# Where the split weight tiles stand, and when the adaLN transfers are issued: one edit to a macaron transformer block

## The chip, the core and the metric

One NeuronCore of a Trainium2 chip runs the whole kernel. The metric is the device time of one execution in microseconds (us); the time before is the median of three runs, 1954.19 us (1942.38, 1954.19 and 1956.5). In the profile PE is TensorE, PEld its weight loads, DVE VectorE, ACT ScalarE, SP the engine whose queue issues the transfers.

## What is computed

One layer for 256 tokens of width 2048, in float32:

```python
mod = silu(c) @ w_ada + b_ada
sh1, sc1, gt1, sh2, sc2, gt2, sh3, sc3, gt3 = split(mod, 9)
h = x + 0.5 * gt1 * swiglu(modulate(rms_norm(x, g_ffn1), sh1, sc1), w1_gate, w1_up, w1_down)
nrm = modulate(rms_norm(h, g_mix), sh2, sc2)
q, k, v = split(nrm @ w_qkv, 3)          # 16 heads of 128: 8 neighbourhood, 8 dilated
...                                      # rms_norm of q and k, attention, rms_norm of the outputs
h = h + gt2 * (concat(o_na, o_dil) @ w_o)
h = h + 0.5 * gt3 * swiglu(modulate(rms_norm(h, g_ffn2), sh3, sc3), w2_gate, w2_up, w2_down)
```

The inner width of both feed-forward parts is 5632 (44 blocks of 128). `w_ada` has 9 x 2048 columns; the kernel calls a block of 128 of them one adaLN item, so there are 144 items of 1 MB.

## The kernel before

**The weight stream.** All large weights come in one fixed order as chunks of 128 x 1024 float32 (512 KB): 12 chunks w1_s, then w1_a (36), w1_b (80), w1_d (64), w1_c (48), w1_e (24), w_qkv (96), w_o (32), w2_a (64), w2_b (64), w2_d (64), w2_c (48), w2_e (24). Letters a, b and c are pieces of the gate and up projections, d and e of the down projection. `wraw` (L138) issues the transfer of a chunk into one of 5 buffers `rw`. For all but the 12 chunks w1_s, `wsplit` (L145) then makes two tiles of it: `hi`, a rounded copy made by ACT (L150), and `lo`, the rest, made by DVE (L151: raw minus hi). Each has 4 buffers (`LOB`), taken in turn. The four `hi` buffers stand one behind another in SBUF, then a spare tile `far` of 192 bytes, then the four `lo` buffers. A buffer has 4096 bytes a partition, so the `lo` of a chunk always stands 4 x 4096 + 192 = 16576 bytes behind its `hi`.

**The matmuls.** In the feed-forward parts and in w_o a chunk holds 8 blocks of 128 x 128. For each, `mm2` (L154) issues a pair of matmuls: `hi` as the stationary operand against 512 columns (an activation's own hi and lo side by side, L156), and `lo` against 256 columns (L157). A chunk is thus 8 pairs. In w_qkv the activations are stationary and the weights move: 12 matmuls of 512 columns a chunk (L162). The order of the instructions on PE is the program's.

**The adaLN items.** `ada_issue` (L119) issues the 1 MB transfer of an item into one of 3 buffers (two `ra`, one `rx`; two in the attention part), `ada_use` (L128) is one DVE instruction over 128 x 2048 (L131) that makes one column of `mods`. Items wait in the list `bg`. `W.chunk` (L296), which fetches three chunks ahead (`AHEAD`), adds `ws.rate` to a credit at each chunk and issues an item for each full credit: `RA` = 0.475 in w1_a, the four numbers of `RB` in w1_b, w1_d, w1_c and w1_e, `RQ` in w_qkv and w_o, `RE` in w2_a, `RF` in the pieces of the second feed-forward part. `bg_until(0)` (L405) stands ahead of w1_e and w2_e: all items have to be issued and used before it in the program. The framework schedules all engines but PE's hand-ordered part: within what data and buffers allow, it may move an instruction forwards or back in its engine's queue, the transfers on SP too.

**Waits.** DVE, ACT and SP each take their queue in order. An `ada_use` whose transfer hasn't landed holds up all that stands behind it on DVE, the `lo` of the next chunk among it.

Of the kernel before, what the change touches and what calls it, by code (L numbers as in the profile page):

```python
# [22 lines left out]
HD = 128  # L23
EPS = 1e-6
NEG = -1e30
CW = 1024
# [10 lines left out]
QS = 1  # L37
PACT = 0
RA = 0.475
RB = (0.1, 0.5, 0.4, 0.15)  # L40
RQ = 0.33
RE = 0.25
RF = (0.1, 0.2, 0.1, 0.1)
AHEAD = 3
# [3 lines left out]
LOB = 4  # L48
URGENT = 400
LINE = 16  # L50
MANUAL = {mybir.EngineType.PE}


# [10 lines left out]
def build(tc, a):  # L64
    nc = tc.nc
    with ExitStack() as ctx:
# [37 lines left out]
        cb = cp.tile([P, D], F32, name="cb")  # L104
        mods = [cp.tile([P, KT], F32, tag=f"m{j}", name=f"m{j}") for j in range(9)]
        nx = [cp.tile([P, 2, S], F32R, tag=f"nx{k}", name=f"nx{k}") for k in range(KT)]

        wide = {}
        turn = [0]
        hold = []  # L110

        def held(ins):
            if hold:
                tc.add_manual_dep(
                    ins.ins, hold[-1].ins.name,
                    mybir.DependencyInfo(mybir.DependencyClass.NoSync, mybir.DependencyReason.DATA),
                    reason="hold")

        def ada_issue(i):  # L119
            turn[0] += 1  # L120
            if wide and turn[0] % (ARA + ARX) >= ARA:
                raw = wide["p"].tile([P, D], F32, tag="arx", bufs=ARX, name=f"rx{i}")
            else:
                raw = wp.tile([P, D], F32, tag="ara", bufs=ARA, name=f"ra{i}")
            nc.sync.dma_start(raw, a["w_ada"][i])
            return raw

        def ada_use(raw, i):  # L128
# [8 lines left out]

        def wraw(src):  # L138
            raw = wp.tile([P, CW], F32, tag="raw", bufs=RAWB, name="rw")
            nc.sync.dma_start(raw, src)  # L140
            return raw

        far = []

        def wsplit(raw):  # L145
            hi = wp.tile([P, CW], F32R, tag="whi", bufs=LOB, name="hiw")
            if not far:
                far.append(wp.tile([P, 3 * LINE], F32, tag="far", bufs=1, name="far"))
            lo = wp.tile([P, CW], F32R, tag="wlo", bufs=LOB, name="low")
            nc.scalar.copy(hi, raw)  # L150
            nc.vector.tensor_tensor(lo, raw, hi.bitcast(F32), ALU.subtract)  # L151
            return hi, lo
# [120 lines left out]
        for nm in ("w1_s", "w1_a", "w1_b", "w1_d", "w1_c", "w1_e", "w_qkv", "w_o",  # L273
                   "w2_a", "w2_b", "w2_d", "w2_c", "w2_e"):
            first[nm] = len(srcs)
            srcs += [a[nm][c] for c in range(a[nm].shape[0])]

        class W:
            def __init__(self):
# [6 lines left out]

            def fetch(self, n):
                while self.head < n:
                    self.ready[self.head] = wraw(srcs[self.head])
                    self.head += 1  # L290

            def whole(self):
# [2 lines left out]

            def chunk(self, ahead=AHEAD):  # L296
                while self.head <= min(self.tail + ahead, len(srcs) - 1):
                    self.ready[self.head] = wsplit(wraw(srcs[self.head]))
# [77 lines left out]
        def ffn(kx, part, ready_k, gate, rates, stat=None, out=None):  # L376
# [120 lines left out]
        hps.close()  # L497

        with tc.tile_pool(name="att", bufs=2) as ap_, tc.tile_pool(name="atc", bufs=1) as ac:
            gq = ac.tile([P, 4, HD], F32, name="gq")  # L500
            nc.sync.dma_start(gq, a["qkg"].partition_broadcast(P))
            rope = ac.tile([P, 2, 2, 32], F32, name="rope")
            nc.sync.dma_start(rope, a["rope"])
            lnc = ac.tile([P, 2, S], F32, name="lnc")
# [18 lines left out]
            def at(u, fn):  # L523
                slots.setdefault(u, []).append(fn)
# [12 lines left out]
                s_["rr"] = rstd_from(s_["ss"], HD, 8, "rq")  # L537

            def qk_norm(g, j, nm, ps, t, s_):
                gi = j + (0 if g < 2 else 2)  # L540
                xn = ap_.tile([P, 4, HD], F32, tag=f"{nm}n{t}", bufs=1, name=f"{nm}n{t}")
                for i in range(4):
                    nc.vector.scalar_tensor_tensor(
                        xn[:, i, :], ps[t][:, i * P : (i + 1) * P],
                        s_["rr"][:, t * 4 + i : t * 4 + i + 1], gq[:, gi, :], ALU.mult, ALU.mult)
# [308 lines left out]
```

## Time and profile before

| what | value |
|---|---|
| median of three runs | 1954.19 us |
| profiled execution, its own time | 1967.14 us |
| its span, first to last instruction | 1965.4 us |
| mean granted TensorE clock | 0.992 |
| PE / DVE / ACT busy | 98% / 80% / 46% of the span |
| bytes moved, mean rate | 503.98 MB, 256 GB/s |

The four runs shown, the profiled one included, lie 25 us apart. Stages in the profile, by the first matmul of each: w1_a from 68 us, w1_b from 181, w1_d from 408, w1_c from 586, w1_e from 727, w_qkv from 802, w_o with the last heads from 1103, w2_a from 1221, w2_b from 1401, w2_d from 1581, w2_c from 1760, w2_e from 1894. A wait is shown as the engine and line that waited, what released it, the sum in us, how often, and the longest. A table by stretches of time counts the instructions that lie in each stretch, those cut by its ends included.

### The profile page before, as it was taken

How to read it: one execution, taken by the hardware profiler on the slowest of the kernel's cores; microseconds unless marked ns; L12 is line 12 of the kernel's file. 1: busy time of each engine (PE TensorE's matmuls, PEld its weight loads, DVE VectorE, ACT ScalarE, POOL GpSimd, SP SyncE). 2: the span in 40 equal slices, each digit the busy share in tenths (PEclk: the TensorE clock that was granted, in tenths of full speed). 3: DMA queues.
4: the chain of work that ended last, by engine and by line, in shares of the span. 5: the costliest groups of instructions: out<-in, count | busy, mean ns of one | idle time of the engine just before them, and what ended most of it. 6: DMA issues, size and time to landing. Idle time of an engine off the chain costs nothing.

```text
span 1965.4 us, 27570 instructions
## 1 busy us (share of the span) xinstructions
PE 1923.0 (98%) x10564; PEld 1659.7 (84%) x10564; DVE 1570.2 (80%) x2122; ACT 906.5 (46%) x1333; POOL 0.7 (0%) x6
## 2 busy tenths in 40 slices
PE   7999999999999999999999999999999999999999
PEld 5878888888887888887888788888888888888888
DVE  7799999998888867989766799988899865555565
ACT  2444544443333454545554555544455443334442
POOL 0000000000000000000000000000000000000000
PEclk8999999999999999999999999999999999999999
DMA  9988888899998976698655445899976666666664
GB/s 383 360 323 296 310 304 306 301 314 337 350 336 322 330 238 202 206 336 306 219 163 165 152 134 170 317 317 334 324 263 191 192 186 189 187 188 188 188 199 133
DMA packets 120083, 503.98 MB, mean 256 GB/s; under 512 B 13328, under 2 KB 15632, under 8 KB 101520
## 3 DMA queue, kind: packets, MB, share of 16 engines
q1 hardware_dynamic: 119952, 502.24, 75.2%
q8 instruction: 82, 1.34, 0.3%
q14 instruction: 49, 0.40, 0.1%
HBM read 500.09 MB, written 2.10 MB: 256 GB/s over the span
## 4 chain that ended last, share of the span: by engine, by line
PE 86%; DVE 7%; DMA 3%; issue 2%; ACT 2%; SPq 0%; DVEq 0%; ACTq 0%
PE pb L156 22%; PE pd L156 15%; PE pb L157 11%; PE pa L156 9%; PE pd L157 7%; PE pqv L162 5%; PE pa L157 5%; PE pqk L162 4%; DVE low L151 3%; PE pa L455 2%; PE pqq L162 2%; DMA ra<-in_w_ada_dram 2%; PE pso L156 2%; DVE ra L131 1%; DMA rx<-in_w_ada_dram 1%
## 5 line engine op out<-in xcount | busy, mean ns | idle before, releaser
L150 ACT CAST hiw<-rw 128x1024 fp32r<-128x1024 f32 x644 | 674.6, 1051 | 793.3 <-PE pd L156 272.0
L151 DVE TENSOR_TENSOR low<-rw,hiw 128x1024 fp32r<-128x1024 f32 x644 | 783.2, 1222 | 246.3 <-ACT hiw L150 243.5
L156 PE MATMUL pb<-nx,hiw 128*128 128x512 f32 x1920 | 676.4, 395 | 0.0
L157 PE MATMUL pb<-nx,low 128*128 128x256 f32 x1920 | 540.1, 281 | 5.3 <-DVE low L151 5.2
L156 PE MATMUL pd<-hd,hiw 128*128 128x512 f32 x1408 | 489.9, 393 | 0.0
L156 PEld LDWEIGHTS pb<-nx,hiw 128*128 128x128 f32 x1920 | 361.1, 188 | 84.7
L157 PE MATMUL pd<-hd,low 128*128 128x256 f32 x1408 | 393.8, 280 | 1.3 <-DVE low L151 1.3
L157 PEld LDWEIGHTS pb<-nx,low 128*128 128x128 f32 x1920 | 363.0, 189 | 6.3 <-DVE low L151 6.3
L156 PEld LDWEIGHTS pd<-hd,hiw 128*128 128x128 f32 x1408 | 264.3, 188 | 59.0
L156 PE MATMUL pa<-nx,hiw 128*128 128x512 f32 x800 | 283.4, 398 | 3.6 <-ACT hiw L150 3.3
L131 DVE CUSTOM_DVE_ANT_0 ra<-ra,cb,vec 128x2048 f32<-128x2048 f32 x101 | 237.2, 2348 | 43.6 <-DMA ra<-in_w_ada_dram 42.9
L157 PEld LDWEIGHTS pd<-hd,low 128*128 128x128 f32 x1408 | 265.8, 189 | 2.2 <-DVE low L151 2.2
L157 PE MATMUL pa<-nx,low 128*128 128x256 f32 x800 | 225.4, 284 | 3.9 <-DVE low L151 3.8
L156 PEld LDWEIGHTS pa<-nx,hiw 128*128 128x128 f32 x800 | 151.1, 190 | 38.9 <-ACT hiw L150 5.2
L157 PEld LDWEIGHTS pa<-nx,low 128*128 128x128 f32 x800 | 153.0, 191 | 8.5 <-DVE low L151 7.5
L131 DVE CUSTOM_DVE_ANT_0 rx<-rx,cb,vec 128x2048 f32<-128x2048 f32 x43 | 101.0, 2348 | 20.3 <-DMA rx<-in_w_ada_dram 20.2
L156 PE MATMUL pso<-ox,hiw 128*128 128x512 f32 x256 | 92.2, 403 | 0.0
L162 PE MATMUL pqk<-hiw,nx 128*128 128x512 f32 x256 | 85.6, 399 | 0.0
L162 PE MATMUL pqq<-hiw,nx 128*128 128x512 f32 x256 | 84.4, 399 | 0.0
L162 PE MATMUL pqv<-hiw,nx 128*128 128x512 f32 x256 | 82.8, 398 | 0.3 <-ACT nx L225 0.3
L370 DVE SCALAR_TENSOR_TENSOR h<-pd,m,h 128x256 f32<-128x256 f32 x128 | 61.3, 482 | 22.5 <-PE pd L157 20.5
L157 PE MATMUL pso<-ox,low 128*128 128x256 f32 x256 | 72.1, 282 | 0.0
(133 smaller groups left out, 1513.0 us busy)
## 6 DMA issues: line engine op xcount, KB each, us to landing
ra<-in_w_ada_dram SPq DMA_DIRECT2D x101, 1024.0 KB, 7.8
rw<-in_w_b_dram SPq DMA_DIRECT2D x144, 512.0 KB, 4.7
rw<-in_w_d_dram SPq DMA_DIRECT2D x128, 512.0 KB, 4.5
rw<-in_w_a_dram SPq DMA_DIRECT2D x100, 512.0 KB, 5.0
rw<-in_w_c_dram SPq DMA_DIRECT2D x96, 512.0 KB, 4.5
rw<-in_w_qkv_dram SPq DMA_DIRECT2D x96, 512.0 KB, 4.1
rx<-in_w_ada_dram SPq DMA_DIRECT2D x43, 1024.0 KB, 7.6
rw<-in_w_e_dram SPq DMA_DIRECT2D x48, 512.0 KB, 4.2
```

What stands on the lines that cost most here:

```text
L131: held(nc.vector.tensor_tensor_reduce(out=raw, in0=raw, in1=cb, scale=1.0, scalar=vec[:, BA + i : BA + i + 1], op0=ALU.mult, op1=ALU.add, ...
L150: nc.scalar.copy(hi, raw)
L151: nc.vector.tensor_tensor(lo, raw, hi.bitcast(F32), ALU.subtract)
L156: nc.tensor.matmul(out, lh, r, start=first, stop=False)
L157: nc.tensor.matmul(out[:, :S], ll, r[:, 0, :], start=False, stop=last)
L162: nc.tensor.matmul(out, l, r, start=first and i == 0, stop=last and i == 2, **kw)
L370: nc.vector.scalar_tensor_tensor(h[d], part_, g, h[d], ALU.mult, ALU.add)
L455: nc.tensor.matmul(pa[f][:, q, :], w[:, b * P : (b + 1) * P], full[k], start=k == 0 and q == 0, stop=k == K1 - 1 and q == 1, skip_group_ch ...
```

## The change

Four edits. First, `hi` and `lo` buffers grow by 64 elements to 4352 bytes, and a chunk's tile begins some elements into its buffer; `PLACE` gives the two offsets (hi, lo) by the chunk's number modulo 8, and w_qkv has (0, 0). The spare tile `far` goes, and a tile `pad` of the same size stands ahead instead. Second, an adaLN transfer gets a scheduling dependence (no semaphore) on the weight transfer issued last in the program, so that it can't be moved ahead of it in SP's queue. Third, `RB` and `RQ` change. Fourth, `bg_until(0)` ahead of w1_e and w2_e is dropped. To make room, the four gain vectors of q and k are loaded as two halves into one smaller tile `gq`; the second half is loaded at unit 56 of the attention part.

```diff
-RB = (0.1, 0.5, 0.4, 0.15)
-RQ = 0.33
+RB = (0.28, 0.36, 0.36, 0.3)
+RQ = 0.2
...
+PLACE = ((12, 36),) + 3 * ((16, 0),) + ((44, 40),) + 3 * ((48, 0),)
...
+        cp.tile([P, 3 * LINE], F32, name="pad")
...
+        queue = []
+
+        def after(ins, other, why):
+            tc.add_manual_dep(
+                ins.ins, other.ins.name,
+                mybir.DependencyInfo(mybir.DependencyClass.NoSync, mybir.DependencyReason.DATA),
+                reason=why)
...
-            nc.sync.dma_start(raw, a["w_ada"][i])
+            ins = nc.sync.dma_start(raw, a["w_ada"][i])
+            if queue:
+                after(ins, queue[-1], "queue")
             return raw
...
             raw = wp.tile([P, CW], F32, tag="raw", bufs=RAWB, name="rw")
-            nc.sync.dma_start(raw, src)
+            ins = nc.sync.dma_start(raw, src)
+            if ws.rate:
+                queue[:] = [ins]
             return raw
 
-        far = []
-
-        def wsplit(raw):
-            hi = wp.tile([P, CW], F32R, tag="whi", bufs=LOB, name="hiw")
-            if not far:
-                far.append(wp.tile([P, 3 * LINE], F32, tag="far", bufs=1, name="far"))
-            lo = wp.tile([P, CW], F32R, tag="wlo", bufs=LOB, name="low")
+        def wsplit(raw, place):
+            hi = wp.tile([P, CW + 64], F32R, tag="whi", bufs=LOB, name="hiw")[:, place[0] : place[0] + CW]
+            lo = wp.tile([P, CW + 64], F32R, tag="wlo", bufs=LOB, name="low")[:, place[1] : place[1] + CW]
             nc.scalar.copy(hi, raw)
             nc.vector.tensor_tensor(lo, raw, hi.bitcast(F32), ALU.subtract)
             return hi, lo
...
-            srcs += [a[nm][c] for c in range(a[nm].shape[0])]
+            for c in range(a[nm].shape[0]):
+                srcs.append((a[nm][c], (0, 0) if nm == "w_qkv" else PLACE[len(srcs) % len(PLACE)]))
...
             ws.pace(rates[3])
-            bg_until(0)
             ffn_down(range(F1, FT), hid, gate, stat, out)
...
-            gq = ac.tile([P, 4, HD], F32, name="gq")
-            nc.sync.dma_start(gq, a["qkg"].partition_broadcast(P))
+            gains = {}
+
+            def gain_load(b):
+                gains["t"] = ac.tile([P, 2, HD], F32, tag="gq", name=f"gq{b}")
+                nc.sync.dma_start(gains["t"], a["qkg"][2 * b : 2 * b + 2].partition_broadcast(P))
+
+            gain_load(0)
...
+            at(56, lambda: gain_load(1))
```

The order of PE's instructions stays as it was; SP, DVE and ACT change theirs from the fourteenth chunk of w1_b on. Two places of SP's queue follow (`rw` is a weight chunk, `ra` and `rx` are adaLN items; x3 means three in a row).

The first chunks of w1_c, before:

```order
L140 DMA rw<-in_w_c_dram 128x1024 x2
L125 DMA rx_5675<-in_w_ada_dram 128x2048
L140 DMA rw<-in_w_c_dram 128x1024 x3
L125 DMA ra_5733<-in_w_ada_dram 128x2048
L140 DMA rw<-in_w_c_dram 128x1024 x2
L125 DMA ra_5802<-in_w_ada_dram 128x2048
L140 DMA rw<-in_w_c_dram 128x1024 x2
L125 DMA rx_5860<-in_w_ada_dram 128x2048
L125 DMA ra_5940<-in_w_ada_dram 128x2048
L140 DMA rw<-in_w_c_dram 128x1024
L125 DMA ra_5987<-in_w_ada_dram 128x2048
L140 DMA rw<-in_w_c_dram 128x1024 x3
```

The same place now:

```order
L149 DMA rw<-in_w_c_dram 128x1024
L132 DMA rx_5045<-in_w_ada_dram 128x2048
L149 DMA rw<-in_w_c_dram 128x1024 x2
L132 DMA ra_5092<-in_w_ada_dram 128x2048
L149 DMA rw<-in_w_c_dram 128x1024 x3
L132 DMA ra_5168<-in_w_ada_dram 128x2048
L149 DMA rw<-in_w_c_dram 128x1024 x3
L132 DMA rx_5248<-in_w_ada_dram 128x2048
L149 DMA rw<-in_w_c_dram 128x1024 x3
L132 DMA ra_5328<-in_w_ada_dram 128x2048
```

Before, three adaLN items stood around a single weight chunk after the ninth chunk of w1_c; now two or three chunks stand between any two items.

The queue at the start of w1_e, before:

```order
L140 DMA rw<-in_w_c_dram 128x1024 x2
L140 DMA rw<-in_w_e_dram 128x1024 x24
L140 DMA rw<-in_w_qkv_dram 128x1024 x8
```

The same place now:

```order
L132 DMA ra_6258<-in_w_ada_dram 128x2048
L149 DMA rw<-in_w_e_dram 128x1024 x3
L132 DMA rx_6327<-in_w_ada_dram 128x2048
L149 DMA rw<-in_w_e_dram 128x1024 x4
L132 DMA ra_6436<-in_w_ada_dram 128x2048
L149 DMA rw<-in_w_e_dram 128x1024 x3
L132 DMA ra_6527<-in_w_ada_dram 128x2048
L149 DMA rw<-in_w_e_dram 128x1024 x4
L132 DMA rx_6630<-in_w_ada_dram 128x2048
L149 DMA rw<-in_w_e_dram 128x1024 x3
L132 DMA ra_6711<-in_w_ada_dram 128x2048
L149 DMA rw<-in_w_e_dram 128x1024 x7
```

Five items now lie among the 24 chunks of w1_e, where there was none.

More of the change, by code (lines that the diff above doesn't have):

```diff
@@ L110, in build @@
         hold = []
+        queue = []
[4 more added lines that the diff above has]
+                reason=why)
         def held(ins):
             if hold:
[L114 to L117, printed above, removed]
+                after(ins, hold[-1], "hold")
         def ada_issue(i):
@@ L288, in fetch @@
                 while self.head < n:
-                    self.ready[self.head] = wraw(srcs[self.head])
+                    self.ready[self.head] = wraw(srcs[self.head][0])
                     self.head += 1
@@ L297, in chunk @@
                 while self.head <= min(self.tail + ahead, len(srcs) - 1):
-                    self.ready[self.head] = wsplit(wraw(srcs[self.head]))
+                    self.ready[self.head] = wsplit(wraw(srcs[self.head][0]), srcs[self.head][1])
                     self.head += 1
@@ L539, in qk_norm @@
             def qk_norm(g, j, nm, ps, t, s_):
-                gi = j + (0 if g < 2 else 2)
                 xn = ap_.tile([P, 4, HD], F32, tag=f"{nm}n{t}", bufs=1, name=f"{nm}n{t}")
@@ L544, in qk_norm @@
                         xn[:, i, :], ps[t][:, i * P : (i + 1) * P],
-                        s_["rr"][:, t * 4 + i : t * 4 + i + 1], gq[:, gi, :], ALU.mult, ALU.mult)
+                        s_["rr"][:, t * 4 + i : t * 4 + i + 1], gains["t"][:, j, :], ALU.mult, ALU.mult)
                 if g >= 2:
```

## The prediction

> **What bounds the kernel now.** I read the page's shares and chain first.
>
> ```profile
> span 1965.4 us, 27570 instructions
> ...
> PE 1923.0 (98%) x10564; PEld 1659.7 (84%) x10564; DVE 1570.2 (80%) x2122; ACT 906.5 (46%) x1333; POOL 0.7 (0%) x6
> ...
> PE 86%; DVE 7%; DMA 3%; issue 2%; ACT 2%; SPq 0%; DVEq 0%; ACTq 0%
> ```
>
> PE makes 86% of the chain that ended last, in a hand-set order that the change leaves alone. Two things can move the end: the pace at which PE runs its matmuls, and the stretches in which it waits (DVE's 7% and DMA's 3%).
>
> The pace comes from a table of stretches, for the first matmul of each pair (L156) alone: PE busy, and in brackets how many lie in the stretch.
>
> ```profile
> core 0: us, PE busy (x) PEld busy (x), PEclk, DMA share, GB/s
> 200.00:400.00 200.00, 200.00 (x567) 106.14 (x567) 1.00 0.87 305
> 460.00:580.00 120.00, 120.00 (x354) 66.24 (x354) 1.00 0.93 343
> 620.00:720.00 100.00, 100.00 (x284) 53.06 (x283) 1.00 0.89 317
> 1240.00:1400.00 160.00, 160.00 (x458) 85.90 (x458) 1.00 0.91 323
> 1420.00:1580.00 160.00, 160.00 (x459) 85.90 (x458) 1.00 0.70 216
> 1600.00:1760.00 160.00, 160.00 (x458) 85.85 (x457) 1.00 0.63 188
> 1780.00:1890.00 110.00, 110.00 (x315) 59.06 (x315) 1.00 0.62 188
> ```
>
> One instruction of each count is cut by the stretch's end, so I divide by one less. The same pair of 512 and 256 columns takes 200/566 = 353.4 ns in w1_b, 120/353 = 339.9 in w1_d, 100/283 = 353.4 in w1_c, and 160/457 = 350.1 all through the second feed-forward part (110/314 = 350.3 at its end). The clock is 1.00 in all, and PE doesn't wait. So PE has three paces: 340, 350 and 353.4. The distance of `lo` behind `hi` was one and the same, 16576 bytes, in all seven rows, so distance alone doesn't set the pace; and the pace doesn't follow the transfers (0.93 of the DMA in the fast row, 0.62 in a slow one). It holds for hundreds of us and differs on the two sides of a wait of PE. [...]
>
> The waits in the first feed-forward part, by what was waited for, first w1_d's beginning (405 to 455 us), then the entry to w1_c (570 to 606 us):
>
> ```profile
> PE pd L157 <- DVE low L151: 1.3, 3, 0.5
> ...
> DVE rx L131 <- DMA rx<-in_w_ada_dram: 6.4, 2, 4.7
> ...
> PE pb L157 <- DVE low L151: 4.6, 1, 4.6
> ```
>
> The 4.6 us can be followed in the order of time on SP and DVE:
>
> ```profile
> 591.20 0.43 SPq L125 DMA_DIRECT2D rx<-in_w_ada_dram  x1
> 591.68 0.42 SPq L125 DMA_DIRECT2D ra<-in_w_ada_dram  x1
> 596.17 0.33 SPq L140 DMA_DIRECT2D rw<-in_w_c_dram  x1
> 596.54 1.56 SPq L125 DMA_DIRECT2D ra<-in_w_ada_dram  x1
> ...
> 600.83 2.35 DVE L131 CUSTOM_DVE_ANT_0 rx<-rx,cb,vec 128x2048 f32<-128x2048 f32 x1 [4.69 <-DMA rx<-in_w_ada_dram]
> 603.11 0.08 DVE L131 DVE_READ_ACCUMULATOR2_ANT m<- 128x1 f32 x1
> 603.11 1.22 DVE L151 TENSOR_TENSOR low<-rw,hiw 128x1024 fp32r<-128x1024 f32 x1
> ```
>
> Two adaLN transfers are issued within 0.5 us, so they share the DMA; the first lands 9.6 us after its issue; DVE stands 4.69 us at its `ada_use`, and the `low` that PE needs is queued behind it. Just after, the granted clock falls:
>
> ```profile
> 604.00:608.00 4.00, 3.62 (x13) 3.08 (x14) 4.00 (x5) 0.00 (x0) 0.00 (x0) 0.64 0.51 186
> ```
>
> Four us at 0.64 of the clock cost 4 x 0.36 = 1.4 us more.
>
> **The transfers, part by part.** The dependence and the new rates take the crowding away: in SP's queue as it now stands, two or three weight chunks lie between any two items of w1_d and w1_c. Gone are 4.6 + 1.4 + 1.3 = 7.3 us, if the items now land in time; the lower bound is 0. I take 7.3: three chunks and one item are 2.5 MB in three chunk times of 2.72 us or more, 308 GB/s, and the fast row shows 343 moved without a wait of PE. The waits in w1_a stay, since its queues are unchanged.
>
> Five items move into w1_e, where there were none, with dropping the deadline. Each is one `ada_use`. DVE in w1_b (200 to 400 us) and in w1_e (727 to 802):
>
> ```profile
> 200.00:400.00 200.00, 193.91 (x263) 1.00 0.87 305
> 727.00:802.00 75.00, 54.34 (x82) 1.00 0.63 194
> ...
> L151 DVE TENSOR_TENSOR low<-rw,hiw 128x1024 fp32r<-128x1024 f32 x71 | 86.6, 1220 | 4.0 <-ACT hiw L150 3.8
> L131 DVE CUSTOM_DVE_ANT_0 ra<-ra,cb,vec 128x2048 f32<-128x2048 f32 x14 | 32.9, 2347 | 0.0
> ...
> L131 DVE CUSTOM_DVE_ANT_0 rx<-rx,cb,vec 128x2048 f32<-128x2048 f32 x6 | 14.1, 2346 | 0.0
> ```
>
> Seven uses in w1_e (two are pending as it begins) are 7 x 2.35 = 16.5 us, and 54.3 + 16.5 = 70.8 still goes into 75: nothing, hidden by DVE's idle time. If that cover is gone, the last two uses stand before the norm of the mixer and cost 4.7 us. In w1_b the items stay what they were: 20 for 71 chunks in the two rows above, 0.28 a chunk, though the table asked for 0.1 (the scheduler had moved them forward); the new table asks for 0.28. In w_qkv the items spread further (0.2 for 0.33). What PE lost there to DVE in the heads is this row (860 to 1110 us):
>
> ```profile
> PE pP L664 <- DVE sc L658: 3.3, 4, 1.6
> ```
>
> Between 0 and 3.3 gained, or as much lost since items now reach into more of the heads; I take 0. The second `gq` transfer waits on SP for the last reader of the first half, four units earlier, which is past: 0. The offsets leave ACT's and DVE's instructions their sizes; were `low` longer than its 1.22 us, DVE has room in all stages but w1_b.
>
> **The distances.** Now `lo` stands 17504, 17344 (three times), 17392, 17216 (three times) bytes behind `hi` over eight chunks, and the tiles' starts move by 48, 64, 176 or 192 bytes; each chunk's first load thus meets the running matmul at other addresses than the load before. Nothing in the trace shows such a chunk. Bounds: at best all slow stretches fall to 340: w1_b 640 pairs, but DVE needs 193.91/71 = 2.73 us a chunk there, so 80 x (2.827 - 2.73) = 7.8 us; w1_c after its first chunk and w1_e, 71 chunks or 568 pairs x 13.4 = 7.6; the second feed-forward part, 264 chunks or 2112 pairs x 10 = 21.1. Together 36.5. At worst all are slow (the third rival). The nearest row is 460 to 580 us: once at 340, PE stayed there through 16 chunk changes in each 44 us, over four buffers. If a lock is only left by a disturbance, a cycle that disturbs it at every chunk can't hold a slow one for 700 us as now; I take it that the two chunks in eight whose offsets aren't multiples of 16 elements do this at half the gain each, and the other six run fast: 7/8 of 36.5 = 31.9 us.
>
> [...]
>
> For w_qkv, with offsets (0, 0), the pieces of the chain are:
>
> ```profile
> 802.10 22.72 PE pqv L162 x96
> 824.82 22.40 PE pqk L162 x96
> 847.22 22.40 PE pqq L162 x96
> ```
>
> 22.40/96 = 233.3 ns for 512 columns. The `lo` stands elsewhere behind `hi` here too: a weight load's step of 6.7 ns (half of 13.4) either way on 1152 matmuls is 7.7 us; I take 0.
>
> **The sum.** The profiled execution took 1967.1 us, 1.7 more than its span: 1967.1 - 7.3 - 31.9 = 1927.9. It lies 12.9 above the median; the runs shown differ by 25 us, which is of the size of the draws of pace, so I make no correction. Forecast: 1928 us, with its own range from 1915 (all at 340, w_qkv a step down: 1967.1 - 7.3 - 36.5 - 7.7) to 1945 (half of the distances' term).
>
> **The rivals.**
> 1. The distances do nothing but draw again. For it: one distance gave three paces. Against: slow paces held for 700 us at the constant distance. With the three paces equally likely the mean is (339.9 + 350.1 + 353.4)/3 = 347.8 ns. The 3320 pairs above then cost 25.9 over 340, for 36.5 now, and the some 390 fast pairs of w1_d lose 3.0: 1967.1 - 7.3 - 7.6 = 1952 us.
> 2. DVE becomes the bound where PE gets fast: w1_b's 2.73 us leaves no room beside PE's 2.72, and every late `low` is a wait; the tail of w1_e pays its 4.7. For it: DVE is 97% busy in w1_b. Against: PE waits for nothing there now. 1928 + 7.8 + 4.7 = 1940 us.
> 3. The cycle locks PE into its slowest pace, since a weight load at some of the new distances collides at every start. For it: most pairs are at 350 or above already. Against: w1_d. The second part loses 2112 x 3.3 = 7.0, w1_d 390 x 13.4 = 5.2, w_qkv its 7.7: 1967.1 - 7.3 + 19.9 = 1980 us. It decides once the collision holds in more than some four of five chunks.
>
> **How the numbers follow.** Forecast 0.56, first rival 0.24, second 0.07, third 0.13. About 1% is what a measurement can tell here: 1934.6 and 1973.7. Faster by over 1%: 0.48 from the forecast, 0.04 from the first rival, 0.02 from the second, 0.54. Slower: 0.10 from the third and 0.01 from the first, 0.11. The rest, 0.35, is within 1%. The range goes from 1905 (a pace below 340 in some chunks) to 1968 (short of the third rival).
>
> **What would show it.** In the table of stretches for L156, w2_b, w2_d and w2_c should show over 465 pairs in 160 us for 458, with no pace that holds for hundreds of us at 350 or 353. PE's wait for `low` at the entry to w1_c should be gone and the clock 1.00 after it. DVE's wait for `rx` and `ra` should shrink in w1_d. If the second part still runs at 350 or 353, the distance step is wrong; if 340 stands in w1_d and the end still doesn't move, look for DVE's `low` in w1_b and at the end of w1_e.

## The result, and the profile after

The change takes the kernel from 1955.35 us (four runs, 1942.38 to 1956.79) to 1929.57 us (four runs, 1926.47 to 1932.2). The ratio is 0.9873, with a 95% interval from 0.9828 to 0.9918. The profiled execution took 1929.37 us; that of before took 1967.14. So the two profiles lie 37.8 us apart and the medians 25.8. The profiled execution of before was 10 us longer than any of its four timed runs, and the record counts it as a slow one, so what the profiles differ by is more than what the change gains.

The span, the shares of the engines and the shares of the chain, from the page of after:

```profile
span 1927.4 us, 27567 instructions
...
PE 1885.8 (98%) x10564; PEld 1639.3 (85%) x10564; DVE 1565.1 (81%) x2122; ACT 906.8 (47%) x1333; POOL 0.7 (0%) x6
...
PE 85%; DVE 8%; DMA 3%; issue 2%; ACT 2%; SPq 0%; DVEq 0%; ACTq 0%
```

PE is as full as before (98%), but it is busy for 37 us less with the same 10564 matmuls, and its weight loads (PEld) are busy for 20 us less. What has shrunk is the time per matmul. The lines of the kernel have moved by 7: the `hi` matmul of a pair is L163 and the `lo` matmul L164, `hi` is made at L157 and `lo` at L158, and an adaLN use is L140. The table of stretches of after for L163, in w1_b, w1_d, w1_c, w2_a, w2_b, w2_d and w2_c:

```profile
core 0: us, PE busy (x) PEld busy (x), PEclk, DMA share, GB/s
200.00:380.00 180.00, 180.00 (x528) 98.83 (x527) 1.00 0.83 297
440.00:560.00 120.00, 120.00 (x352) 65.88 (x352) 1.00 0.92 334
610.00:700.00 90.00, 90.00 (x264) 49.40 (x264) 1.00 0.90 324
1210.00:1360.00 150.00, 150.00 (x439) 82.30 (x439) 1.00 0.80 292
1385.00:1535.00 150.00, 149.38 (x438) 81.88 (x437) 1.00 0.68 221
1560.00:1710.00 150.00, 147.70 (x432) 80.90 (x432) 1.00 0.72 262
1740.00:1850.00 110.00, 110.00 (x323) 60.43 (x322) 1.00 0.65 193
```

With one instruction cut by a stretch's end, a pair now takes 180/527 = 341.6 ns, 120/351 = 341.9, 90/263 = 342.2, 150/438 = 342.5 and 110/322 = 341.6. Before, it took 353.4, 339.9, 353.4 and 350.1 in these stages: the three paces are gone, and one mean pace stands everywhere. In the sixth row PE isn't quite full (147.70 of 150), and the fifth lacks 0.6; that is a wait, below.

The start of each chunk's first matmul in the trace shows what the mean is made of. At the eight places of the cycle, from (12, 36) on, a chunk's eight pairs take 2784, 2721, 2720, 2724, 2769, 2720, 2720 and 2722 ns (medians in w1_d; the other pieces of the feed-forward parts that run undisturbed show the same to 1 ns). 2720 ns is the fast pace (340 a pair); the slow ones are 2800 and 2827.

PE's waits in the whole span, as the list of waits has them (us in total, times, the longest):

```profile
PE pP L675 <- DVE sc L669: 5.9, 3, 2.6
...
PE pd L164 <- DVE low L158: 1.8, 2, 1.0
...
PE pb L164 <- DVE low L158: 1.1, 2, 0.7
```

The 4.6 us at the entry to w1_c are gone. But PE's wait in the attention heads has grown from 3.3 to 5.9 us, and two waits of 1 us have come into w2_d, where there was none. The cause of these two shows in the list of waits of 1540 to 1727 us:

```profile
DVE ra L140 <- DMA ra<-in_w_ada_dram: 26.6, 7, 5.0
DVE rx L140 <- DMA rx<-in_w_ada_dram: 16.3, 4, 5.2
```

DVE stands 42.9 us here for adaLN items; before, it was 12.1 us in the whole of w2_a to w2_c (1210 to 1900 us). One of these in the order of time, on SP and on DVE:

```profile
1633.52 0.42 SPq L132 DMA_DIRECT2D rx<-in_w_ada_dram  x1
...
1641.81 2.35 DVE L140 CUSTOM_DVE_ANT_0 rx<-rx,cb,vec 128x2048 f32<-128x2048 f32 x1 [4.80 <-DMA rx<-in_w_ada_dram]
...
1644.48 4.62 DVE L158 TENSOR_TENSOR low<-rw,hiw 128x1024 fp32r<-128x1024 f32 x4
```

The item is issued at 1633.5 us and its use starts 8.3 us later; DVE had nothing to do for 4.80 of it in queue order, and then makes four `low` in a row, which had been held up.

Stage by stage (from the first matmul of one to that of the next, the last stage to the end of its last matmul), the two profiled executions in us against the prediction's own terms:

| stage | before | after | difference | predicted |
|---|---|---|---|---|
| w1_a | 112.7 | 109.4 | -3.3 | 0 |
| w1_b | 227.2 | 220.2 | -7.0 | -6.8 (7/8 of 7.8) |
| w1_d | 177.4 | 175.0 | -2.4 | -1.3 |
| w1_c and w1_e | 216.3 | 203.9 | -12.4 | -12.6 (4.6 + 1.4, and 7/8 of 7.6) |
| w_qkv | 301.2 | 302.1 | +0.9 | 0 |
| w_o | 117.7 | 117.7 | 0 | 0 |
| second feed-forward part | 740.5 | 727.6 | -12.9 | -18.5 (7/8 of 21.1) |

The rows add up to -37.1, for -39.2 predicted; the rest of the 37.8 lies ahead of w1_a.

### The profile page after: what moved, and what is told of

Same layout as the page of the kernel before. It is cut to its first block, busy times and chain, and to the rows that moved or that the text cites. A ratio compares the mean times of both kernels' runs of the same rounds, so it can differ in the third digit from the quotient of the medians.

```text
span 1927.4 us, 27567 instructions
## 1 busy us (share of the span) xinstructions
PE 1885.8 (98%) x10564; PEld 1639.3 (85%) x10564; DVE 1565.1 (81%) x2122; ACT 906.8 (47%) x1333; POOL 0.7 (0%) x6
## 4 chain that ended last, share of the span: by engine, by line
PE 85%; DVE 8%; DMA 3%; issue 2%; ACT 2%; SPq 0%; DVEq 0%; ACTq 0%
PE pb L163 20%; PE pd L163 17%; PE pb L164 10%; PE pd L164 8%; PE pa L163 8%; PE pqk L169 4%; PE pa L164 4%; PE pqv L169 3%; DVE low L158 3%; PE pqq L169 3%; DMA ra<-in_w_ada_dram 2%; PE pa L462 2%; PE pso L163 2%; ACT hiw L157 1%; PE pso L164 1%
## 5 line engine op out<-in xcount | busy, mean ns | idle before, releaser
L157 ACT CAST hiw<-rw 128x1024 fp32r<-128x1024 f32 x644 | 674.2, 1049 | 705.1 <-PE pd L163 234.0
L158 DVE TENSOR_TENSOR low<-rw,hiw 128x1024 fp32r<-128x1024 f32 x644 | 782.0, 1221 | 186.5 <-ACT hiw L157 184.5
L163 PE MATMUL pb<-nx,hiw 128*128 128x512 f32 x1920 | 657.4, 390 | 0.0
L164 PE MATMUL pb<-nx,low 128*128 128x256 f32 x1920 | 532.1, 277 | 1.1 <-DVE low L158 1.1
L163 PE MATMUL pd<-hd,hiw 128*128 128x512 f32 x1408 | 481.9, 390 | 0.0
L163 PEld LDWEIGHTS pb<-nx,hiw 128*128 128x128 f32 x1920 | 360.5, 188 | 76.9
L164 PE MATMUL pd<-hd,low 128*128 128x256 f32 x1408 | 390.1, 277 | 1.8 <-DVE low L158 1.8
L164 PEld LDWEIGHTS pb<-nx,low 128*128 128x128 f32 x1920 | 360.9, 188 | 1.9 <-DVE low L158 1.9
L163 PEld LDWEIGHTS pd<-hd,hiw 128*128 128x128 f32 x1408 | 264.3, 188 | 56.3
L140 DVE CUSTOM_DVE_ANT_0 ra<-ra,cb,vec 128x2048 f32<-128x2048 f32 x101 | 237.2, 2349 | 75.2 <-DMA ra<-in_w_ada_dram 75.0
L163 PE MATMUL pa<-nx,hiw 128*128 128x512 f32 x800 | 276.1, 392 | 3.7 <-ACT hiw L157 3.2
L164 PEld LDWEIGHTS pd<-hd,low 128*128 128x128 f32 x1408 | 264.6, 188 | 2.6 <-DVE low L158 2.4
L164 PE MATMUL pa<-nx,low 128*128 128x256 f32 x800 | 221.6, 279 | 4.0 <-DVE low L158 4.0
L163 PEld LDWEIGHTS pa<-nx,hiw 128*128 128x128 f32 x800 | 149.6, 188 | 37.2 <-ACT hiw L157 5.2
L164 PEld LDWEIGHTS pa<-nx,low 128*128 128x128 f32 x800 | 150.4, 188 | 8.9 <-DVE low L158 7.9
L140 DVE CUSTOM_DVE_ANT_0 rx<-rx,cb,vec 128x2048 f32<-128x2048 f32 x43 | 101.0, 2348 | 28.6 <-DMA rx<-in_w_ada_dram 28.3
L163 PE MATMUL pso<-ox,hiw 128*128 128x512 f32 x256 | 92.4, 404 | 0.0
L378 DVE SCALAR_TENSOR_TENSOR h<-pd,m,h 128x256 f32<-128x256 f32 x128 | 61.2, 481 | 16.5 <-PE pd L164 14.7
L164 PE MATMUL pso<-ox,low 128*128 128x256 f32 x256 | 72.5, 283 | 0.0
```

The source lines that it names most:

```text
L140: held(nc.vector.tensor_tensor_reduce(out=raw, in0=raw, in1=cb, scale=1.0, scalar=vec[:, BA + i : BA + i + 1], op0=ALU.mult, op1=ALU.add, ...
L163: nc.tensor.matmul(out, lh, r, start=first, stop=False)
L164: nc.tensor.matmul(out[:, :S], ll, r[:, 0, :], start=False, stop=last)
L378: nc.vector.scalar_tensor_tensor(h[d], part_, g, h[d], ALU.mult, ALU.add)
```

## The experiments

Two theories stood against each other at first. **By address** (the "lock theory" of the expectations): a pace, once taken, stays; which pace it is depends on how far `lo` stands behind `hi`, and the cycle of distances keeps PE from staying in a slow one. **By the transfers:** the slow paces come from waits and crowding, and the better order of the transfers brings the gain. Later a third came in: **any disturbance in time** would do.

Experiments 1 to 4 ran on one chip, 5 to 8 on one, 9 to 11 on one, and 12 by itself, each time beside runs of the kernel before, whose medians were 1959.6, 1959.9, 1955.5 and 1959.4 us. A ratio is always to these, with its 95% interval in brackets; medians of different groups are better compared by their ratios.

**1. The transfers alone** (`transfers_alone`). The change with the old tiles:

```diff
-PLACE = ((12, 36),) + 3 * ((16, 0),) + ((44, 40),) + 3 * ((48, 0),)
+PLACE = ((0, 0),)
...
+            hi = wp.tile([P, CW], F32R, tag="whi", bufs=LOB, name="hiw")
+            if not far:
+                far.append(wp.tile([P, 3 * LINE], F32, tag="far", bufs=1, name="far"))
+            lo = wp.tile([P, CW], F32R, tag="wlo", bufs=LOB, name="low")
```

> The changed kernel with the tiles as they stood before: lo always 16576 bytes behind hi, no cycle; dependence, rates and dropped deadline as changed. Lock theory (only the cycle of distances makes PE fast): the waits at the entry to w1_c are gone, but the feed-forward parts run for hundreds of us at one pace drawn by chance, 340, 350 or 353 ns a pair; about 1947 us (1935 to 1955), and 350 or 353 in at least one stretch of over 100 us. Rival (fewer waits of PE are what keeps it fast): 340 nearly everywhere and 1930 us or less.

Measured: 1958.44 us (10 runs, 1939.4 to 1964.0), ratio 0.9985 [0.9954, 1.0017]. The median lies 3.4 us above the range that was expected. The wait at the entry to w1_c is gone here too, and yet nothing is gained. The table of stretches for its `hi` matmul (w1_b, w1_d, w2_b):

```profile
200.00:380.00 180.00, 180.00 (x516) 96.65 (x515) 1.00 0.82 292
440.00:560.00 120.00, 120.00 (x344) 64.43 (x343) 1.00 0.90 324
...
1400.00:1530.00 130.00, 130.00 (x372) 69.69 (x372) 1.00 0.66 217
```

180/515 = 349.5 ns, 120/343 = 349.9, 130/371 = 350.4. From 184.9 us on 1709 pairs in a row ran at 350, w1_d among them, which had run at 340 before with the same tiles. A constant distance thus holds a pace for hundreds of us, and another execution can hold another.

**2. The places alone** (`places_alone`). The cycle of distances with the old rates, no dependence and the old deadline:

```diff
-RB = (0.28, 0.36, 0.36, 0.3)
-RQ = 0.2
+RB = (0.1, 0.5, 0.4, 0.15)
+RQ = 0.33
...
-            if queue:
-                after(ins, queue[-1], "queue")
...
+            bg_until(0)
```

> The changed kernel with the cycle of distances, but the old rates, no dependence on the weight transfer and the old deadline. Lock theory: the paces of the changed kernel chunk by chunk (six of eight at 2.72 us, one at 2.78 and one at 2.77), while the wait of some 4 to 5 us at the entry to w1_c with its 1.4 us of low clock is back: 1935 us (1931 to 1940). Rival (the transfers did it): stretches of 350 or 353 as before, 1950 to 1957.

Measured: 1928.41 us (1926.54 to 1929.02), ratio 0.9834 [0.9818, 0.9851]. This is the whole gain of the change, without its transfers, and 2.6 us below the range that was expected. The rows of w1_d, w2_b and w2_d, then PE's waits:

```profile
440.00:560.00 120.00, 119.21 (x350) 65.35 (x349) 1.00 0.92 339
1385.00:1535.00 150.00, 149.91 (x439) 82.23 (x439) 1.00 0.71 233
1560.00:1710.00 150.00, 150.00 (x440) 82.37 (x439) 1.00 0.63 194
```

```profile
PE pb L162 <- DVE low L156: 3.9, 4, 2.0
...
PE pd L162 <- DVE low L156: 2.1, 3, 1.1
```

The waits of the first feed-forward part are back, though not as expected: the longest at the entry to w1_c is 2.0 us and the clock stays at 1.00. w1_d takes 178.3 us and w1_c 135.8, together 7.8 more than in the change (175.0 and 131.3), of which 5.3 are PE's waits in the two. But w_qkv takes 297.2 for 302.1, w2_b 175.2 for 176.1 and w2_d 175.0 for 177.7, together 8.5 less. So the transfers gain about as much in one place as they lose in three others.

**3. One place for all chunks** (`one_place`), a constant distance of 17344 bytes instead of the constant 16576 of before:

```diff
-PLACE = ((12, 36),) + 3 * ((16, 0),) + ((44, 40),) + 3 * ((48, 0),)
+PLACE = ((16, 0),)
```

> The changed kernel with one pair of offsets for all chunks, (16, 0), so lo stands 17344 bytes behind hi always. Lock theory (a change of distance is what frees PE): slow stretches of over 100 us are back, 1940 us (1930 to 1950). Rival (17344 is simply a better distance than 16576): 2.72 us in all chunks, without the two slower chunks in eight of the cycle, 68 x (0.064 + 0.049) = 8 us less than the changed kernel: 1922.

Measured: 1953.36 us (10 runs, 1938.78 to 1960.69), ratio 0.9956 [0.9927, 0.9986]. The slow stretches are back as expected; the median lies 3.4 us above the expected range. The rows of w1_b, w1_d, w2_b and w2_c of the profiled execution (its 1938.78 us are the fastest of the ten):

```profile
200.00:380.00 180.00, 180.00 (x531) 99.43 (x530) 1.00 0.82 298
440.00:560.00 120.00, 120.00 (x354) 66.24 (x353) 1.00 0.92 339
...
1400.00:1530.00 130.00, 130.00 (x373) 69.80 (x372) 1.00 0.69 229
...
1760.00:1850.00 90.00, 90.00 (x256) 47.76 (x255) 1.00 0.59 186
```

All three paces at one distance once more: 180/530 = 339.6 ns and 120/353 = 339.9 in the first part, 130/372 = 349.5 in w2_b, 90/255 = 352.9 in w2_c. In the trace 1708 pairs in a row run at 340 from 185 us on, 1440 at 350 from 1199, and 644 at 353 from 1704.6, where PE had waited for a moment. So the distance that three in eight of the change's chunks have doesn't by itself keep PE fast.

**4 and 5. One odd place in eight** (`one_kick`, `kick_44_40`):

```diff
-PLACE = ((12, 36),) + 3 * ((16, 0),) + ((44, 40),) + 3 * ((48, 0),)
+PLACE = ((12, 36),) + 7 * ((16, 0),)
```

```diff
+PLACE = ((44, 40),) + 7 * ((48, 0),)
```

> The changed kernel with (12, 36) for one chunk in eight and (16, 0) for the other seven. Lock theory: one disturbance in eight chunks is enough, the odd chunk takes 2.78 us and the other seven 2.72, 68 x 0.049 = 3.3 us less than the changed kernel: 1926. Rival (all eight distances are needed, each frees PE from a pace that the one before leaves): 2.80 us in some stretches of over 50 us, 1933 or more.

> The changed kernel with (44, 40) for one chunk in eight and (48, 0) for the other seven. Theory (each of the two odd chunks frees PE from one slow pace: in the run with (12, 36) alone 350 held through it, and in the changed kernel a 350 ends at the (44, 40) chunk): no stretch of 350 over 8 chunks; 353 may hold; if it frees from both, 1929 - 68 x 0.064 = 1925 us. Rival (only the pair of odd chunks together works): 350 for hundreds of us, 1936 us or more.

Measured: 1936.95 us (1930.81 to 1940.55), ratio 0.9878 [0.9855, 0.99], and 1920.98 us (1919.63, 1920.98 and 1931.79), ratio 0.9816 [0.9763, 0.9869]. For w1_d and w2_b, first of `one_kick`, then of `kick_44_40`:

```profile
440.00:560.00 120.00, 120.00 (x353) 65.98 (x353) 1.00 0.91 337
1400.00:1530.00 130.00, 130.00 (x373) 69.83 (x372) 1.00 0.70 230
```

```profile
440.00:560.00 120.00, 120.00 (x353) 66.08 (x352) 1.00 0.93 340
1400.00:1530.00 130.00, 128.29 (x377) 70.47 (x377) 1.00 0.69 226
```

(12, 36) alone does half of it, and the time is the rival's, not the theory's 1926: twice in its trace a chunk at 353 meets it, and 340 follows, but the second part runs at 350 throughout (130/372 = 349.5), its odd chunk taking 2805 ns and the seven others 2799 to 2802. (44, 40) brings PE back from 350: its own chunk takes 2831 ns, the next 2745, and then 2720. No chunk at 353 met it in this profile; in those of `places_alone` and `rate_only` a few did, and they took 2768 or 2769, 2745 and then 2720. No slow stretch in the profile of `kick_44_40` lasts over eight chunks. (The profiled execution is the longest of its three: 1.7 us of waits lie in the 130 us of its second row.)

**6. Multiples of 64 bytes only** (`whole_lines`). The distance changes four times in eight chunks, and every offset is a multiple of 16 elements, which are 64 bytes (the kernel's `LINE`):

```diff
+PLACE = ((0, 32),) + 3 * ((16, 0),) + ((32, 48),) + 3 * ((48, 0),)
```

> The changed kernel with a cycle of eight whose offsets are all multiples of 16 elements, (0, 32), 3 x (16, 0), (32, 48), 3 x (48, 0), so the distance of lo behind hi changes as in the changed kernel, but each tile starts at the same place within 64 bytes. Theory (the start within 64 bytes frees PE): slow paces hold for hundreds of us, median 1940 to 1960 us, over 10 us between single runs. Rival (a change of the distance between hi and lo frees it): no slow stretch over eight chunks, 1925 to 1932 us.

Measured: 1946.57 us (7 runs, 1942.52 to 1952.09), ratio 0.9937 [0.9909, 0.9964]. From 1778 to 1804 us DVE waits for ACT's `hi` ahead of each `low` (10 times of 10, 11.6 us in all), and in the order of time the starts of `low` step by the chunks' lengths:

```profile
1781.64 1.23 DVE L158 TENSOR_TENSOR low<-rw,hiw 128x1024 fp32r<-128x1024 f32 x1 [1.50 <-ACT hiw L157]
...
1784.44 1.23 DVE L158 TENSOR_TENSOR low<-rw,hiw 128x1024 fp32r<-128x1024 f32 x1 [0.97 <-ACT hiw L157]
...
1787.27 1.23 DVE L158 TENSOR_TENSOR low<-rw,hiw 128x1024 fp32r<-128x1024 f32 x1 [0.81 <-ACT hiw L157]
...
1790.10 1.22 DVE L158 TENSOR_TENSOR low<-rw,hiw 128x1024 fp32r<-128x1024 f32 x1 [1.27 <-ACT hiw L157]
1792.92 1.23 DVE L158 TENSOR_TENSOR low<-rw,hiw 128x1024 fp32r<-128x1024 f32 x1 [1.60 <-ACT hiw L157]
...
1795.70 1.23 DVE L158 TENSOR_TENSOR low<-rw,hiw 128x1024 fp32r<-128x1024 f32 x1 [0.95 <-ACT hiw L157]
...
1798.43 1.23 DVE L158 TENSOR_TENSOR low<-rw,hiw 128x1024 fp32r<-128x1024 f32 x1 [0.70 <-ACT hiw L157]
...
1801.14 1.23 DVE L158 TENSOR_TENSOR low<-rw,hiw 128x1024 fp32r<-128x1024 f32 x1 [1.16 <-ACT hiw L157]
1803.86 1.23 DVE L158 TENSOR_TENSOR low<-rw,hiw 128x1024 fp32r<-128x1024 f32 x1 [1.49 <-ACT hiw L157]
```

The steps are 2.80, 2.83, 2.83, 2.82, 2.78, 2.73, 2.71 and 2.72 us, and so through all stages: by place, from (0, 32) on, the chunks take 2810, 2827, 2827, 2821, 2775, 2721, 2720 and 2720 ns. (0, 32) puts PE into the slowest pace, (32, 48) into the fastest, wherever PE doesn't wait. So moves by multiples of 64 bytes do switch the pace, and the cycle can switch it either way. No theory had both halves of this: the slow stretches are broken up, as the one had it, and half of all chunks are slow all the same.

**7. The starts move, the distance doesn't** (`same_distance`). Both tiles of a chunk are shifted alike:

```diff
+PLACE = ((12, 12),) + 3 * ((0, 0),) + ((44, 44),) + 3 * ((32, 32),)
```

> The changed kernel with offsets that are equal for hi and lo, (12, 12), 3 x (0, 0), (44, 44), 3 x (32, 32): lo stands 17408 bytes behind hi in every chunk, while two chunks in eight start 48 bytes off the 64-byte grid of the others. Theory (the start within 64 bytes frees PE, the distance is nothing): no slow stretch over eight chunks, 1925 to 1935 us. Rival (the distances do it): slow paces for hundreds of us, 1940 to 1960 us.

Measured: 1954.97 us (9 runs, 1952.35 to 1959.01), ratio 0.9977 [0.9955, 0.9998]. Rows of w1_d and w2_b:

```profile
440.00:560.00 120.00, 120.00 (x345) 64.39 (x344) 1.00 0.91 328
1400.00:1530.00 130.00, 130.00 (x373) 69.76 (x373) 1.00 0.67 219
```

120/344 = 348.8 ns and 130/372 = 349.5. By place the chunks take 2781, 2778, 2773, 2775, 2810, 2814, 2807 and 2802 ns in every stage: here too the addresses fix the pace, though the distance never changes, and the executions lie within 7 us. So the starts count as well as the distance. But none of the eight places gets to 2720: at this distance, moving the starts doesn't make PE fast. Whether another constant distance would do with moving starts, and whether 17408 bytes can hold 340 with the starts at rest, was not run.

**8. Later items untied** (`half_tied`). The change with the dependence ended after the first feed-forward part, and w_qkv's rate set back:

```diff
-RQ = 0.2
+RQ = 0.33
...
+        tie = [True]
...
-            if ws.rate:
+            if ws.rate and tie[0]:
...
+        tie[0] = False
+        queue.clear()
```

> The changed kernel with the dependence of the adaLN transfers ended after the first feed-forward part, and w_qkv's old rate 0.33. Theory (the changed transfers gain some 8 us in w1_d and w1_c and give them back in w_qkv and in w2_b and w2_d): w_qkv takes 297 us for 302, w2_b and w2_d 175 each for 176 and 178, the median is 1921 us (1918 to 1925). Rival (those losses are chance of the profiled execution): 1927 to 1931.

Measured: 1918.7 us (1918.17 to 1925.26), ratio 0.9796 [0.9757, 0.9836]. w_qkv takes 297.1 us, w2_b 175.1 and w2_d 175.0, while w1_d and w1_c keep their 175.0 and 131.3. In w2_d PE is full again:

```profile
1560.00:1710.00 150.00, 150.00 (x439) 82.31 (x440) 1.00 0.65 193
```

DVE waits for no item in w2_d here. This keeps what the transfers gain and drops what they cost, as experiment 2 had it.

**9. The rate alone** (`rate_only`): `RQ` back to 0.33, the dependence kept.

```diff
-RQ = 0.2
+RQ = 0.33
```

> The change with the rate in w_qkv and w_o set back from 0.2 to 0.33, the dependence kept everywhere. half_tied undid both, and got w_qkv 5.0 us shorter, w2_b 1.0 and w2_d 2.7. If the rate is the cause in w_qkv (at 0.2 the adaLN uses spread into more of the heads): w_qkv at 297 us, w2_b and w2_d as in the change or shorter since fewer items are left for them; about 1923 to 1925 us. If the dependence is the cause: w_qkv at 302, and 1929 us.

Measured: 1921.15 us (1920.59 to 1923.99), ratio 0.9837 [0.9803, 0.9871]; w_qkv takes 295.9 us, w2_b 175.0 and w2_d 179.0. DVE's wait for items in w_qkv and PE's wait in the heads, from its lists of waits:

```profile
DVE ra L140 <- DMA ra<-in_w_ada_dram: 3.8, 4, 1.5
```

```profile
PE pP L675 <- DVE sc L669: 3.7, 3, 2.0
```

In the change the first was 14.7 us. So the rate costs w_qkv its 5 us: in all profiles with the tiles moved, w_qkv takes 295.9 to 297.6 us at 0.33 (four of them) and 299.7 to 303.6 at 0.2 (eight). The wait in w2_d stays, and w2_d takes 1.3 us more than in the change, against what was expected. It belongs to the dependence: `half_tied` differs from this run in nothing else, and has none.

**10. Both together** (`best_both`): `half_tied` with the cycle of `kick_44_40`.

```diff
-PLACE = ((12, 36),) + 3 * ((16, 0),) + ((44, 40),) + 3 * ((48, 0),)
+PLACE = ((44, 40),) + 7 * ((48, 0),)
```

> half_tied (1918.7 us) with the cycle of kick_44_40: one chunk in eight with (44, 40), the other seven at (48, 0). Theory (a cycle is the sum of its places): by places the cycle of the change costs 64 + 1 + 4 + 49 + 2 = 120 ns in eight chunks over 8 x 2720, this one 49; 71 ns x 548/8 cycles = 4.9 us less, so 1914 us, with w_qkv at 297 us and w2_b and w2_d at 174.5. Rival (one odd place in eight leaves a slow stretch standing longer after a wait than two do, and this eats the 4.9): 1918 us or more, and chunks of 2800 or 2827 ns in the profile over more than eight in a row.

Measured: 1916.97 us (1914.99 to 1918.5), ratio 0.9816 [0.9791, 0.9842]. Added up over the feed-forward stages its profile is 3.9 us shorter than that of `half_tied` (1429.2 for 1433.1), and its longest slow stretch has 38 pairs, under five chunks. In the time of the whole kernel 1.7 us isn't told from nothing, by the ratios it is no faster at all (0.9816 for 0.9796), and its w_o took 117.2 for 115.5. So the sum by places holds in the stages, and whether the kernel as a whole gains by it stays open. The change's own ratio is 0.9873 [0.9828, 0.9918].

**11 and 12. A disturbance without moving the tiles** (`bare_disturbance`, `three_times_as_often`). `one_place` with an extra matmul of 128 columns ahead of a new accumulation, whose result the next matmul overwrites:

```diff
+        since = [0]
...
+            since[0] += 1
+            if first and since[0] > 64:
+                since[0] = 0
+                tc.keep_in_program_order(
+                    nc.tensor.matmul(out[:, :P], nx[0][:, 0, :P], nx[0][:, 0, :P], start=True, stop=True))
```

> one_place (constant distance of 17344 bytes) with one extra matmul of 128 columns, which computes nothing that is used, ahead of every ninth chunk or so: a disturbance in time with no change of address. Theory (the pace is a lock, and only an odd relation of addresses lets PE out of a slow one; a shift in time alone redraws it at most): all three paces appear, changing at the extra matmuls or not at all, and stretches of 2800 or 2827 ns a chunk stand over most of some stages; 1940 to 1960 us, the extra matmuls themselves taking 548/9 x 0.06 to 0.1 = 4 to 6 us of it. Rival (any disturbance frees PE to 340, and the cycle is only one way to give it): chunks of 2720 ns throughout, 1921 + 5 = about 1926 us.

Measured: 1936.37 us (9 runs, 1923.61 to 1950.02), ratio 0.9908 [0.9876, 0.994]. The median lies where neither theory had put it. The profiled execution ran at 340 in nearly all its pairs; four times PE came to an extra matmul at 350, and three times it went on at 340 (the fourth time a wait followed). That spoke for the rival, the spread of 26 us against it. So the last run tripled the extra matmuls (`> 64` became `> 16`).

> bare_disturbance with the extra matmul ahead of each new accumulation after 16 pairs instead of 64: 170 extra matmuls for 57, some 0.06 us each, so 10 us for 3.4, and still one distance of 17344 bytes. bare_disturbance ran from 1923.6 to 1950.0 us; in its profiled execution nearly all pairs were at 340 ns, and the few clear slow stretches ended at the next extra matmul. Theory (the extra matmul lets PE out of a slow pace with some chance each time): three times as many chances leave slow stretches of a few chunks at most, so the executions draw together, 1930 to 1938 us. Rival (the extra matmul is no way out: in the fast execution the lock had been drawn at 340 at the starts, and in the slow ones slow stretches stand through the extra matmuls): the spread stays at 20 us or more, with a median near 1943, and a slow stretch in the profile goes on past several extra matmuls.

Measured: 1953.19 us (10 runs, 1946.21 to 1962.85), ratio 0.9973 [0.995, 0.9996]. The median is above what either theory expected, and the runs lie 17 us apart, less than the rival's 20; its slow stretch past several extra matmuls is there. In w2_d and w2_c, first the `hi` matmuls, then the extra ones:

```profile
1590.00:1740.00 150.00, 149.79 (x426) 79.83 (x425) 1.00 0.73 255
1760.00:1880.00 120.00, 119.82 (x340) 63.77 (x340) 1.00 0.61 185
```

```profile
1590.00:1740.00 150.00, 2.90 (x13) 2.44 (x13) 1.00 0.73 255
1760.00:1880.00 120.00, 2.45 (x11) 2.06 (x11) 1.00 0.61 185
```

As an estimate, an extra matmul of 128 columns costs a quarter of the 226.7 ns that one of 512 takes in w_qkv, 0.06 us; with 13 of these off, 149.2/425 = 351 ns: in the trace the pairs between two extra matmuls run at 350 from 1545 us to the end, past more than 30 of them. Comparing the four pairs ahead of each extra matmul with four behind it, 350 went on 58 times and gave way to 340 six times; 340 went on 88 times. So an extra matmul can let PE out of a slow pace but mostly doesn't. Why it did in `bare_disturbance`, whose runs went down to 1923.6 us, isn't explained; its ratio isn't told apart from that of `one_place`.

## Why the prediction came out, point by point

**What it said would show it.** 438 pairs in 150 us of w2_b are 467 in 160, and 323 in 110 us of w2_c are 470: over 465, as forecast. w2_d has 432 in 150, 461 in 160, which falls short, by its new waits. The wait at the entry to w1_c is gone. DVE's waits for items fell from 26.2 us to 11.4 over w1_d. At its very beginning they grew, from 2.6 us to 4.9 in some 50 us, but PE no longer waits there. (The 6.4 us for `rx` that the prediction shows belong to the entry to w1_c, not to w1_d.)

**A constant distance holds a pace: shown. What holds it: not shown.** `one_place` and `transfers_alone` hold one pace for 1440 to 1709 pairs in a row. w1_d ran at 340 before and at 350 in `transfers_alone`, with the same tiles. That the pace is drawn anew in each execution of one kernel fits the 22 and 25 us between their runs, but only one execution of each has a trace. The 31.9 us rested on the author's assumption that a slow pace is a lock that only a disturbance ends, and no run shows that; what the runs show in its place is a pace that goes with the place of a chunk's two tiles (2720 to 2827 ns a chunk in one execution of `whole_lines`).

**A lock "only left by a disturbance", and two odd chunks in eight for it: right in the outcome, too wide in the reason.** The eight chunk lengths of after are what the step took: two odd ones near half gain (2784 and 2769 ns between 2720 and 2827), six fast (2720 to 2724). But an extra matmul is a disturbance too, and 350 went on past 30 of it; shifting both tiles alike is one, and no chunk got fast. Among the cycles, only those that change the distance of `lo` behind `hi` too brought chunks to 2720, and the place decides where PE ends: (44, 40) and (32, 48) bring 340 (chunks of 2720 ns follow), (0, 32) brings 353 (2827 ns), (12, 36) frees from 353 only (350 went on at 2799 to 2802 ns). As each such cycle moves the starts as well, no run tells the distance by itself from the two addresses together. That the offsets aren't multiples of 16 elements, which the prediction gave as the reason for the two odd chunks, isn't what matters: multiples of 16 switch as well. Why one place is good and another bad stays open.

**The size of the distances' term, 31.9 us: near.** The first part gave what was forecast (w1_b -7.0 for -6.8), and 1.1 more in w1_d, whose first pairs had run at 353 before, which the sum left out. The second gave 12.9 for 18.5. `half_tied` splits the 5.6 that are missing: without the waits for items the second part takes 724.6 us, 3.0 less than in the change; of the other 2.6, the mean chunk explains 1.1 (2735 ns, where 2801 less 7/8 of 80 is 2731, for 264 chunks), and 1.5 stay unexplained.

**w1_a's 3.3 us: the clock of one execution.** They were left out of the sum, and aren't the change's. The first 20 us of the stage, for the `hi` matmul, before and after:

```profile
70.00:90.00 20.00, 19.71 (x50) 10.73 (x50) 0.85 0.92 340
```

```profile
70.00:90.00 20.00, 19.75 (x58) 10.69 (x58) 1.00 0.98 385
```

At 0.85 of the clock, 20 us lose 3.0. `transfers_alone`, with the old tiles, has 1.00 there and takes 109.9 us for w1_a, as the change does (109.4).

**w1_b's limit by DVE: not reached.** `one_place` ran w1_b at 339.6 ns a pair with DVE busy for 178 of 180 us and PE waiting for nothing, so DVE keeps up to that point. The second rival, for which this was the place, didn't come about.

**The transfers' 7.3 us: the size was right, the zeros beside it weren't.** (The 308 GB/s that the prediction sets against 343 are 321: three chunks and an item are 2.62 MB in 8.16 us. It still fits.) Against `places_alone` the change gains 7.8 us in w1_d and w1_c. The clock of 0.64 after the entry to w1_c is gone with the wait (from 560 to 600 us the clock is 1.00 and PE full). But `RQ` = 0.2 was costed at 0 with bounds of 3.3, and what the dependence does in the second feed-forward part wasn't looked at. Two stretches of 40 us in w_qkv, all engines, of after:

```profile
860.00:900.00 40.00, 37.95 (x185) 31.60 (x184) 30.17 (x43) 19.28 (x34) 0.00 (x0) 0.96 0.71 253
...
980.00:1020.00 40.00, 36.33 (x163) 29.57 (x162) 31.62 (x66) 18.06 (x40) 0.00 (x0) 0.96 0.60 197
```

Spread further, the items reach into the heads, where DVE waits 14.7 us for them; PE's wait for `sc` grows by 2.6 us, and PE is idle for some 2 and 3.7 us of these stretches. The granted clock falls to a mean of 0.96 in them, which is, as an estimate, 2 x 40 x 0.04 = 3.2 us more; before, it was 1.00 from 864 to 1076 us. Over the whole of w_qkv PE is busy 2.8 us longer than in `half_tied` with the same matmuls, and idle 2.2 us longer, which makes the 5.0. That is the same pair of losses, a wait and then a lower clock, that the change had removed at the entry to w1_c: PE is busy for 1.95 us of 870 to 874 and the clock is 0.69 from 874 to 878, and for 1.35 us of 988 to 992 and the clock is 0.57 from 992 to 996.

**w_qkv's 0: two errors that cancelled.** The matmuls of w_qkv did take the step down that the prediction kept as a bound of 7.7 us. The pieces of the chain of after:

```profile
776.16 22.15 PE pqv L169 x96
798.31 21.76 PE pqk L169 x96
```

21.76/96 = 226.7 ns, for 233.3 before. The stage would have become 4 to 5 us shorter, and does so in `places_alone` (297.2) and `rate_only` (295.9); the rate gave it back. Hence +0.9 in the table.

**The median: in part luck.** The sum was made against an execution 12.9 us above the median, without a correction. For the paces that was sound, since the change removes their draw, whatever it was: its runs lie within 6 us, those of before within 14. But the low clock of w1_a was in that execution too and wasn't to come back. That the forecast of 1928 us lies 1.6 from the median rests on errors that cancel: 3.3 (w1_a) and 1.1 (w1_d) more was gained than forecast, and 5.6 (second part) and 0.9 (w_qkv) less. The first rival (1952 us) and the third (1980) are out by the result, though `transfers_alone` (1958.4) and `one_place` (1953.4) show that the first is what happens with one distance, and (0, 32) of `whole_lines`, after which the chunks take 2827 ns, that a place can put PE into its slowest pace, as the third had it.

**The first rival's premise, that the distances do nothing but draw again: not borne out.** One execution of `whole_lines` has chunks of 2720 and of 2827 ns, by place, so PE's pace does depend on where its two weight tiles stand. Why it does, no run here shows.

## What to carry to other kernels

Where two matmuls alternate and one pair's time differs between stages at full clock and without a wait (here 340, 350 and 353 ns at 1.00), look at the addresses of the tiles before looking at the transfers (here the places alone gave a ratio of 0.9834, the transfers alone 0.9985), and time several executions, since one profile shows one draw (those of `transfers_alone` lay 25 us apart). A rate or a dependence that mends one stage acts in all stages that it covers: check each of them for the engine that stands at a late transfer (here DVE, for 14.7 us in w_qkv and 42.9 us between 1540 and 1727 us), and end the rule where it stops paying (`half_tied`: w_qkv 5.0 and w2_d 2.7 us shorter than in the change, ratio 0.9796 for 0.9873).

## What was unexpected of the hardware

One distance gives three stable paces for the same pair (340, 350 and 353 ns), of which 340 and 350 outlasted 1700 pairs, 353 at least 644, and 350 outlasted 58 of 64 extra matmuls; the executions of one such kernel then lie 15 to 26 us apart (before, `transfers_alone`, `one_place` and the two with extra matmuls). Where the tiles' places cycle, they lie 2.5 to 12 us apart (the change and the eight other versions), and that holds for `same_distance` too, where the distance doesn't change. In w_qkv, too, where the weights are the moving operand, moving the tiles took a matmul of 512 columns from 233.3 to 226.7 ns: all twelve profiles with the larger buffers show 226.7, the two with the old ones 231.1 and 233.3.
